# An encoder layer on one core: VectorE's wide additions and subtractions of SBUF operands issued with an accumulator output

## The chip, the cores and the metric

The kernel runs on one core of a Trainium2 chip. The metric is the device time of one execution in microseconds (us), the median of 3 runs. Engines: TensorE (PE, matrix products), VectorE (DVE), ScalarE (ACT), GpSimd (POOL) and SyncE (SP, which issues most of the DMAs).

## The reference

One layer of a streaming encoder, for a prompt of 1024 frames and for 32 new frames whose 512 predecessors are in caches. Shared weights, model width 1024, 8 + 8 heads of 64, inner width 4096, all float32:

```python
h = rmsnorm(x, g_mix)
q_a, k_a, v_a, q_i, k_i, w_i, q_b, k_b, v_b, gate_a, gate_b = split(h @ w_in)
# mixer A: q_a, k_a normed and rotated; an indexer scores every earlier frame,
score = sum_h relu(q_i @ k_i.T) * w_i         # the best 256 (sample: 136) are attended
# mixer B: stick-breaking attention, strictly causal
a = exp(log_sigmoid(z) - tail)
m = sigmoid(gate_a) * (o_a @ w_branch_a) + sigmoid(gate_b) * (o_b @ w_branch_b)
h = x + m @ w_out
y = h + square(relu(rmsnorm(h, g_ffn) @ w_up)) @ w_down
```

The outputs are y and the new keys and values of both mixers, for both groups.

## The kernel before, in words

Activations lie transposed, features on the 128 partitions and the 1056 frames (1024 + 32) along the columns. A float32 product is made of three matmuls on halves: x = xh + xl and w = wh + wl, where xh is x rounded to the matmul's type fp32r and xl the rest. `three` (L500) issues xh·wh, xl·wh and xh·wl into one PSUM bank. The halves are made by two engines: ScalarE casts (`copy`) into the high half, and VectorE or GpSimd subtracts it from the source to give the low half, both operands in SBUF. For a tile of weights (128 x 512) these are the names wst or raw (as loaded), wh and wl; rb is a second such source. GpSimd does most of the weights' subtractions in the first stages and VectorE a part of them.

The stages: the input projections and the indexer (to about 450 us, interleaved), attention of both mixers per head, then `branch`, `out` and the feed-forward part for the frames in two groups of columns, g1 (512 columns) and g2 (544 columns, in chunks of 272). The feed-forward part of g2 is computed with 7 products of quarter matrices in place of 8, so it adds and subtracts weights and activations beforehand (names rw, sl, more, il, gl, ul); sums of weights are made earlier and kept in DRAM (ws, dw_up, dw_down).

Three places that the following speaks of:

- `project_a` (L1247) makes the queries and keys of mixer A. Of each chunk of columns it squares the projection (sq), adds the squares of both halves of a head on GpSimd, casts the sum on ScalarE into the first half of a tile az and subtracts on VectorE into the second (L1301). TensorE sums over the head's rows with small matmuls `t<-heads,az` of 4 columns, first on the high half, then on the low one.
- `branch` (L1623) is the multiplication with the branch matrices. For mixer A its `done` multiplies on VectorE (pb<-pj,sg), adds the other branch on GpSimd (pb<-pb,y), casts on ScalarE (xh<-pb) and subtracts on VectorE (xl<-pb,xh, L1647). The tiles of these halves, mh and ml, lie in xh1 and xl1. Each of 8 row blocks e has two chunks of 272 columns.
- `out` (L1652) is the product with W_out: for each of 8 blocks of output rows and each chunk it accumulates over k = 0..7, and so needs the row blocks k of `branch`. k = 6 and 7 are the last that `branch` makes.

No instruction is issued where it is written. Every call goes through the class `Plan`: `record` (L303) notes the instruction, its rank and its dependences; `cost` (L237) gives its length by a formula of its engine, operation and columns; `run` and `issue` (L379, L414) then write the order, engine by engine: what is ready by the planner's own clock, the lowest rank first (URGENT, FAST, PREP, MAIN, FILL, SLOW), then the order of recording. All instructions therefore have line L436, that of the call in `issue`. The planner also keeps the shared access of VectorE and GpSimd to SBUF: `locks` (L294) says whether a VectorE instruction needs it (every GpSimd instruction does), and `issue` shifts an instruction behind the other engine's one that has it. In `cost`, a plain addition of n columns has 150 + 1.06 n ns, `tensor_tensor_reduce` 230 + 1.05 n, and `locks` says no for the latter. While `dense` is set (the feed-forward part of g2), VectorE's costs of operands outside PSUM are taken 1.3 times.

`tensor_tensor_reduce` is used in two places before the change: in `softmax_weights` (p<-s,mask; s in PSUM), and in the indexer's selection (L1142, pen<-pen,score; both in SBUF), whose accumulator outputs are read by later work.

Of the kernel before, what the change touches and what calls it, by code (L numbers as in the profile page):

```python
# [9 lines left out]
F32 = mybir.dt.float32  # L10
F32R = mybir.dt.float32r
# [3 lines left out]
ALU = mybir.AluOpType  # L15
# [72 lines left out]
class Mem:  # L88


    def __init__(self, parts, words, old=(), floor=0.0):
        self.writer = np.full((parts, words), -1, np.int32)
        self.readers = []
        self.old, self.floor = old, floor
        self.touched = []
# [14 lines left out]

TABLE = {AF.Exp: "exp", AF.Sigmoid: "sigmoid", AF.Sqrt: "sqrt"}
PE, DVE, ACT, POOL, SP = range(5)
SLACK, STORE = 300, 1000
CHANGE = 20


class Plan:
# [3 lines left out]
    def __init__(self, nc, tc):  # L121
        self.nc, self.tc = nc, tc
        self.tensor, self.vector = Issuer(self, PE, nc.tensor), Issuer(self, DVE, nc.vector)
        self.scalar, self.gpsimd = Issuer(self, ACT, nc.scalar), Issuer(self, POOL, nc.gpsimd)
        self.sync = Issuer(self, SP, nc.sync)
        self.nodes, self.mem, self.rings = [], {}, {}
        self.members, self.banks, self.onchip = {}, set(), set()
        self.floors = {"left": 0.0, "right": 0.0, None: 0.0}
        self.free = [0.0] * 5
        self.now = [[] for _ in range(5)]  # L130
        self.later = [[] for _ in range(5)]
        self.pipe = 0.0
        self.port = {DVE: (0.0, 0.0), POOL: (0.0, 0.0)}
        self.table = None
        self.row = None
        self.patience = 0
        self.level = [2]
        self.hold = None
        self.dense = False


    @contextmanager
# [94 lines left out]
    def cost(self, eng, op, out, ins, scalar, kw):  # L237
        n = 1
        for s in out.shape[1:]:
            n *= s  # L240
        if eng == PE:
            rhs = ins[1]
            cols = 1
            for s in rhs.shape[1:]:
                cols *= s
            stat = 1
            for s in ins[0].shape[1:]:
                stat *= s
            four = 4 if op == "matmul" and rhs.dtype == F32 else 1
            occ = four * max((cols + 29) / 2.4, stat / 1.2 + 2 if stat > 64 else 60)  # L250
            return occ, occ + 175
        if eng == DVE:
            if op == "reciprocal":
                d = 160 + 6.2 * n
            elif op == "tensor_tensor_scan":
                d = 160 + 2.06 * n
            elif op in ("tensor_scalar", "tensor_scalar_mul"):
                d = 160 + 1.0 * n + (80 if "accum_out" in kw else 0)
            elif op == "tensor_tensor_reduce":
                d = 230 + 1.05 * n  # L260
            elif op == "scalar_tensor_tensor":
                d = 155 + (1.06 if isinstance(scalar, (int, float)) else 1.2) * n
            elif op == "reduce_sum":
                k = 1
                for s in ins[0].shape[1:]:
                    k *= s
                d = 150 + 1.05 * k
            elif op == "memset":
                d = 100 + 0.3 * n
            elif op == "tensor_copy":  # L270
                d = 160 + 0.62 * n
            else:
                d = 150 + 1.06 * n
            if self.dense and not any(x.tensor.name in self.banks for x in ins):
                d *= 1.3
            return d - 70, d
        if eng == ACT and op != "dma_start":
            d = 195 + 0.84 * n + (190 if "accum_out" in kw else 0)
            if op == "activation" and any(not isinstance(kw.get(k, 0.0), (int, float)) for k in ("scale", "bias")):
                d += 100  # L280
            return d - 90, d
        if op == "dma_start" and eng == POOL:
            return 1000.0, 1000.0
        if eng == POOL:
            d = 300 + 0.9 * n if op in ("tensor_scalar", "memset") else 330 + 1.9 * n
            if op == "tensor_scalar" and out.dtype == F32R:
                d = 230 + 3.2 * n
            if self.dense:
                d *= 1.05
            return d - 30, d  # L290
        d = 470.0 if out.shape[0] > 64 else 620.0
        return d, d
# [9 lines left out]

    def record(self, eng, fn, op, args, kw):  # L303
        args = list(args)
        out = kw["out"] if "out" in kw else args[0]
        outs = [out] + ([kw["accum_out"]] if kw.get("accum_out") is not None else [])
        rest = args[1:] if "out" not in kw else args
        ins = [x for x in rest if isinstance(x, bass.AP)]
        ins += [x for k, x in kw.items() if isinstance(x, bass.AP) and k not in ("out", "accum_out")]
        reads = list(ins)  # L310
        if op == "copy_predicated":
            reads.append(out)
        n = Node()
        n.id, n.eng, n.call = len(self.nodes), eng, (fn, args, kw)
        n.key = (self.level[-1], n.id)
        n.occ, n.lat = self.cost(eng, op, out, ins, args[2] if op == "scalar_tensor_tensor" else None, kw)
        n.size = 0
        n.table = TABLE.get(args[2]) if op == "activation" else None
        n.store = op == "dma_start" and out.tensor.name not in self.onchip and self.level[-1] != FAST
        if op == "dma_start":  # L320
            n.size = 4
            for s in max((out, ins[0]), key=lambda z: z.size()).shape:
                n.size *= s
            if (out if out.tensor.name in self.onchip else ins[0]).shape[0] <= 64:
                n.size *= 1.6
        n.lock = eng == POOL or eng == DVE and self.locks(op, out, ins, args)
        n.row = out.tensor.name if eng == PE and self.level[-1] == FILL else None
        n.wait = self.patience
        n.succ, n.need, n.ready, n.end, n.start = [], 0, 0.0, None, None
        self.nodes.append(n)  # L330
        deps = set()
        found = []
        for aps, write in ((reads, False), (outs, True)):
            for ap in aps:
                c = self.cells(ap)
                if c is None:
                    continue
                m, part, idx = c
                w = m.writer[part, idx]
                if (w < 0).any():  # L340
                    deps.update(m.old)
                    n.ready = max(n.ready, m.floor)
                deps.update(np.unique(w).tolist())
                if write:
                    for r, rpart, ridx in m.readers:
                        if rpart.start < part.stop and part.start < rpart.stop and self.meet(idx, ridx, m.writer.shape[1]):
                            deps.add(r)
                found.append((m, part, idx, write))
        for m, part, idx, write in found:
            if write:  # L350
                m.writer[part, idx] = n.id
                if m.writer.shape == (1, 1):
                    m.readers = []
            else:
                m.readers.append((n.id, part, idx))
            if not m.touched or m.touched[-1] != n.id:
                m.touched.append(n.id)
        if eng == SP and self.hold is not None:
            deps.add(self.hold)
        deps.discard(-1)  # L360
        deps.discard(n.id)
        for d in deps:
            d = self.nodes[d]
            if d.end is not None:
                n.ready = max(n.ready, self.after(d, n))
            else:
                d.succ.append(n)
                n.need += 1
        if not n.need:
            heapq.heappush(self.later[eng], (n.ready, n.id))  # L370
# [74 lines left out]
class Layer:  # L445
# [114 lines left out]
    def run(self):  # L560
        nc, a = self.nc, self.a
# [8 lines left out]
        c = lambda shape, dt, name: nc.tile(self.const, shape, dt, name)  # L570
# [14 lines left out]
        self.vl = c([128, 4, 8], F32, "vl")  # L585
        self.gf = c([128, KB], F32, "gf")
        self.ngf = c([128, KB], F32, "ngf")

        dt = lambda shape, name: nc.tile(self.dram, shape, F32, name)
        self.dq = dt([2 * H, 2, HD, T], "dq")  # L590
# [1807 lines left out]
```

## Time and profile before

| | |
|---|---|
| median of 3 runs | 1673.52 us (1671.99 to 1674.35) |
| profiled execution | 1678.86 us, of which the span is 1677.1 |
| granted TensorE clock | 0.999 of full speed |
| busy: TensorE | 1662.6 us |
| busy: VectorE, 2577 instructions | 1212.8 us |
| busy: ScalarE | 1086.8 us |
| busy: GpSimd | 1061.6 us |

Times in the views are us from the span's start unless marked ns. A row of the timeline gives start, duration, engine, line, operation, output<-inputs, the shape (partitions x columns), and in brackets how long the engine had been idle and what ended that. A row of the groups gives the count, the busy time in all, the mean ns of one, and the idle time ahead with its releaser. In names, numbers of tiles are left out; they stand in the rows of the order below.

### The profile page before, as it was taken

How to read it: one execution, taken by the hardware profiler on the slowest of the kernel's cores; microseconds unless marked ns; L12 is line 12 of the kernel's file. 1: busy time of each engine (PE TensorE's matmuls, PEld its weight loads, DVE VectorE, ACT ScalarE, POOL GpSimd, SP SyncE). 2: the span in 40 equal slices, each digit the busy share in tenths (PEclk: the TensorE clock that was granted, in tenths of full speed). 3: DMA queues.
4: the chain of work that ended last, by engine and by line, in shares of the span. 5: the costliest groups of instructions: out<-in, count | busy, mean ns of one | idle time of the engine just before them, and what ended most of it. 6: DMA issues, size and time to landing. Idle time of an engine off the chain costs nothing.

```text
span 1677.1 us, 34259 instructions
## 1 busy us (share of the span) xinstructions
PE 1662.6 (99%) x11584; PEld 1564.8 (93%) x11584; DVE 1212.8 (72%) x2577; ACT 1086.8 (65%) x2389; POOL 1061.6 (63%) x914
## 2 busy tenths in 40 slices
PE   9999999999999999999999999999999999999999
PEld 9999999898999998989888889999999999999998
DVE  6557778999947656899888766676646783767577
ACT  7656698893235577667677666576844775747472
POOL 3366676876555266563576567778877884646563
PEclk9999999999999999999999999999999999999999
DMA  7378797745377679666597375657865656565664
GB/s 253 118 208 276 256 291 253 253 167 175 127 238 192 173 203 244 201 186 188 173 314 249 120 236 159 210 170 222 281 200 169 202 166 183 170 179 167 177 204 156
DMA packets 208339, 339.96 MB, mean 203 GB/s; under 512 B 32650, under 2 KB 62202, under 8 KB 208163
## 3 DMA queue, kind: packets, MB, share of 16 engines
q1 hardware_dynamic: 207874, 337.64, 66.1%
q8 instruction: 91, 1.49, 0.4%
q14 instruction: 86, 0.70, 0.1%
q10 hardware_dynamic: 288, 0.13, 0.0%
HBM read 249.80 MB, written 87.77 MB: 201 GB/s over the span
## 4 chain that ended last, share of the span: by engine, by line
PE 92%; DVE 5%; ACT 1%; issue 1%; POOL 1%; DMA 0%; SPq 0%; DVEq 0%; POOLq 0%; ACTq 0%
PE pj L436 65%; PE s L436 13%; PE o L436 5%; PE t L436 5%; PE pd L436 4%; DVE p L436 1%; DVE junk L436 0%; ACT junk L436 0%; DVE az L436 0%; DVE t L436 0%; DVE sl L436 0%; DVE rwq L436 0%; DVE pj L436 0%; DVE pre L436 0%; DVE more L436 0%
## 5 line engine op out<-in xcount | busy, mean ns | idle before, releaser
L436 PE MATMUL pj<-xh,wh 128*128 128x272 f32 (+2 forms) x1624 | 527.3, 326 | 3.5 <-ACT part L436 3.2
L436 PE MATMUL pj<-xl,wh 128*128 128x272 f32 (+2 forms) x1624 | 527.0, 326 | 0.0
L436 PE MATMUL pj<-xh,wl 128*128 128x272 f32 (+2 forms) x1624 | 526.7, 325 | 0.0
L436 POOL TENSOR_TENSOR wl<-wst,wh 128x512 fp32r<-128x512 f32 (+1 forms) x232 | 325.6, 1408 | 224.8 <-ACT wh L436 191.3
L436 PEld LDWEIGHTS pj<-xh,wh 128*128 128x128 f32 x1624 | 305.9, 189 | 23.6 <-ACT part L436 3.4
L436 PEld LDWEIGHTS pj<-xl,wh 128*128 128x128 f32 x1624 | 306.2, 189 | 19.1
L436 PEld LDWEIGHTS pj<-xh,wl 128*128 128x128 f32 x1624 | 305.9, 189 | 19.2
L436 ACT CAST wh<-wst 128x512 fp32r<-128x512 f32 (+1 forms) x260 | 160.0, 619 | 147.8 <-PE pj L436 107.2
L436 POOL TENSOR_TENSOR wl<-raw,wh 128x512 fp32r<-128x512 f32 x77 | 104.8, 1364 | 43.5 <-ACT wh L436 43.2
L436 PE MATMUL pj<-gl,wh 128*128 128x272 f32 (+1 forms) x444 | 126.8, 286 | 0.0
L436 PE MATMUL pj<-gh,wh 128*128 128x272 f32 (+1 forms) x444 | 126.6, 286 | 0.0
L436 PE MATMUL pj<-gh,wl 128*128 128x272 f32 (+1 forms) x444 | 126.2, 286 | 0.0
L436 DVE TENSOR_TENSOR tt<-t,tt 128x512 fp32r<-128x512 f32 (+2 forms) x168 | 101.2, 620 | 32.4 <-ACT tt L436 30.9
L436 ACT ACTIVATE junk<-score,cand 128x384 bf16<-128x384 f32 (+1 forms) x124 | 116.0, 936 | 6.0 <-DVE cand L436 4.0
L436 ACT CAST tt<-t 128x512 fp32r<-128x512 f32 (+2 forms) x168 | 87.2, 538 | 38.6 <-PE o L436 18.4
L436 ACT CAST wh<-raw 128x512 fp32r<-128x512 f32 x122 | 75.9, 624 | 53.0 <-PE pj L436 30.6
L436 DVE TENSOR_TENSOR_SCAN p<-p,seen 128x384 f32<-128x384 f32 (+3 forms) x64 | 104.7, 1659 | 4.5 <-ACT p L436 4.4
L436 PE MATMUL o<-tt,v 128*128 128x256 f32 (+1 forms) x640 | 102.7, 279 | 1.1 <-DVE o L436 1.0
L436 PEld LDWEIGHTS o<-tt,v 128*128 128x128 f32 x640 | 94.0, 189 | 10.2 <-DVE o L436 1.3
L436 POOL TENSOR_TENSOR ws<-ws 128x512 f32<-128x512 f32 x64 | 83.0, 1297 | 20.1 <-issue 8.8
L436 PE MATMUL s<-k,q 128*128 128x384 f32 (+5 forms) x384 | 93.9, 350 | 0.0
L436 PE MATMUL t<-ident,p 128*128 128x128 f32 x596 | 89.9, 274 | 0.0
(509 smaller groups left out, 4505.3 us busy)
## 6 DMA issues: line engine op xcount, KB each, us to landing
q<-dq SPq DMA_DIRECT2D x64, 256.0 KB, 4.1
raw<-w_down SPq DMA_DIRECT2D x51, 256.0 KB, 3.0
ws<-w_up SPq DMA_DIRECT2D x48, 256.0 KB, 4.4
dw_up<-ws SPq DMA_DIRECT2D x48, 256.0 KB, 3.4
k<-dk SPq DMA_DIRECT2D x48, 256.0 KB, 4.7
v<-dv SPq DMA_DIRECT2D x48, 256.0 KB, 3.7
raw<-dw_up SPq DMA_DIRECT2D x45, 256.0 KB, 3.0
wst<-w_up SPq DMA_DIRECT2D x44, 256.0 KB, 2.9
```

What stands on the lines that cost most here:

```text
L436: fn(*args, **kw)
```

## The change

In `record`, VectorE's `tensor_add` and `tensor_sub` of two-dimensional tiles of at least 256 columns, with no operand in PSUM, are issued as `tensor_tensor_reduce`: the same addition or subtraction elementwise into the same output, and a running maximum over the columns into one column of a new constant tile, `low`. Nothing reads `low`, and the planner isn't told that it is written. The planner then costs and places these instructions by its rules for `tensor_tensor_reduce`, without shared access and without the factor 1.3.

```diff
+COUNTED = {"tensor_add": ALU.add, "tensor_sub": ALU.subtract}
+LEAST, ROUNDED = 256, True
...
-            if self.dense and not any(x.tensor.name in self.banks for x in ins):
+            if self.dense and op != "tensor_tensor_reduce" and not any(x.tensor.name in self.banks for x in ins):
                 d *= 1.3
...
     def record(self, eng, fn, op, args, kw):
         args = list(args)
+        if eng == DVE and op in COUNTED and self.junk is not None:
+            out, x, y = args
+            if len(out.shape) == 2 and out.shape[1] >= LEAST and not any(z.tensor.name in self.banks for z in args):
+                if out.dtype != F32R or ROUNDED:
+                    fn, args = self.nc.vector.tensor_tensor_reduce, []
+                    kw = dict(out=out, in0=x, in1=y, scale=1.0, scalar=0.0, op0=COUNTED[op], op1=ALU.max,
+                              accum_out=self.junk[:out.shape[0]])
+                    op = "tensor_tensor_reduce"
         out = kw["out"] if "out" in kw else args[0]
-        outs = [out] + ([kw["accum_out"]] if kw.get("accum_out") is not None else [])
+        acc = kw.get("accum_out")
+        outs = [out] + ([acc] if acc is not None and (self.junk is None or acc.tensor.name != self.junk.tensor.name) else [])
...
+        nc.junk = c([128, 2], F32, "low")[:, 0:1]
```

259 of VectorE's instructions are concerned: 91 make low halves of weights wl, about 40 low halves xl of activations, 50 sums of weights, 23 more, 16 sl, 12 az, and the rest gl, ha, il and the like. Each becomes two instructions, in the order's words `ISA wl,low<-wst,wh 128x512` and `ISA low 128x1`, the second of which writes the accumulator to `low`. VectorE's instructions in the order are 2735 in place of 2476. The other engines' numbers are the same, but the order is planned anew: of the instructions that stand elsewhere in the order, outside the longest common sequence, TensorE has about 1,400 of some 11,575 (by up to 122 places), VectorE and ScalarE about 420 each, GpSimd about 130, and SyncE 246 (by up to 22 places), nearly all from 290 us on.

Two places, first the product with W_out for g2, at about 1284 us. TensorE before: k = 4 and 5 of the bank pj_16882 (first chunk of one block of output rows), and the beginning of pj_16885 (the second chunk); xh1 and xl1 are the halves of the activations, wh_16880 and wl_16881 the weights of k = 4 to 7.

```order
L436 MATMUL pj_16882<-xh1_227,wh_16880 128x272
L436 MATMUL pj_16882<-xl1_228,wh_16880 128x272
L436 MATMUL pj_16882<-xh1_227,wl_16881 128x272
L436 MATMUL pj_16882<-xh1_227,wh_16880 128x272
L436 MATMUL pj_16882<-xl1_228,wh_16880 128x272
L436 MATMUL pj_16882<-xh1_227,wl_16881 128x272
L436 MATMUL pj_16885<-xh1_227,wh_16877 128x272
L436 MATMUL pj_16885<-xl1_228,wh_16877 128x272
```

TensorE now, the same place from k = 5 on; the numbers of the tiles are 4 higher (pj_16886 is the first chunk's bank, pj_16889 the second's) and the activations are xh1_228 and xl1_229.

```order
L448 MATMUL pj_16886<-xh1_228,wh_16884 128x272
L448 MATMUL pj_16886<-xl1_229,wh_16884 128x272
L448 MATMUL pj_16886<-xh1_228,wl_16885 128x272
L448 MATMUL pj_16886<-xh1_228,wh_16884 128x272
L448 MATMUL pj_16886<-xl1_229,wh_16884 128x272
L448 MATMUL pj_16886<-xh1_228,wl_16885 128x272
L448 MATMUL pj_16889<-xh1_228,wh_16881 128x272
L448 MATMUL pj_16889<-xl1_229,wh_16881 128x272
L448 MATMUL pj_16889<-xh1_228,wl_16882 128x272
L448 MATMUL pj_16889<-xh1_228,wh_16881 128x272
L448 MATMUL pj_16886<-xh1_228,wh_16884 128x272
L448 MATMUL pj_16889<-xl1_229,wh_16881 128x272
```

Before, the second chunk starts right after k = 5 of the first, and k = 6 of the first begins 26 matmuls later; now k = 6 follows k = 5 at once, and the first matmul of k = 7 stands four matmuls into the second chunk. GpSimd before, at the same place: pb_16865 and pb_16867 are the two chunks of `branch` that become k = 6, pb_16873 and pb_16875 those of k = 7; the rows wl split weights.

```order
L436 TENSOR_TENSOR wl_16892<-wst_16890,wh_16891 128x512
L436 TENSOR_TENSOR wl_16900<-wst_16898,wh_16899 128x512
L436 TENSOR_TENSOR pb_16865<-pb_16865,y1_16204 128x272
L436 TENSOR_TENSOR pb_16867<-pb_16867,y1_16204 128x272
L436 TENSOR_TENSOR pb_16873<-pb_16873,y1_16204 128x272
L436 TENSOR_TENSOR wl_16903<-wst_16901,wh_16902 128x512
L436 TENSOR_TENSOR pb_16875<-pb_16875,y1_16204 128x272
```

GpSimd now, tile numbers again 4 higher (y1 is 5 lower).

```order
L448 TENSOR_TENSOR pb_16869<-pb_16869,y1_16199 128x272
L448 TENSOR_TENSOR pb_16871<-pb_16871,y1_16199 128x272
L448 TENSOR_TENSOR wl_16896<-wst_16894,wh_16895 128x512
L448 TENSOR_TENSOR pb_16877<-pb_16877,y1_16199 128x272
L448 TENSOR_TENSOR pb_16879<-pb_16879,y1_16199 128x272
L448 TENSOR_TENSOR wl_16904<-wst_16902,wh_16903 128x512
```

The additions of k = 6 now stand ahead of both splits of weights, and those of k = 7 between them.

The second place is `project_a` at about 319 us. TensorE before: t_4191 sums az_4190 with the matrix heads; s_4224 and s_4225 are the projections in progress.

```order
L436 MATMUL s_4224<-xh0_225,wl_4216 128x512
L436 MATMUL t_4191<-heads_74,az_4190 128x4 x4
L436 MATMUL t_4191<-heads_74,az_4190 32x4 x2
L436 MATMUL s_4225<-xh0_225,wh_4218 128x512
L436 MATMUL s_4225<-xl0_226,wh_4218 128x512
L436 MATMUL s_4225<-xh0_225,wl_4219 128x512
```

TensorE now, where az_4191 and t_4192 are the same tiles.

```order
L448 MATMUL t_4192<-heads_74,az_4191 128x4
L448 MATMUL s_4226<-xh0_226,wh_4219 128x512
L448 MATMUL s_4226<-xl0_227,wh_4219 128x512
L448 MATMUL s_4226<-xh0_226,wl_4220 128x512
L448 MATMUL s_4226<-xh0_226,wh_4219 128x512
L448 MATMUL s_4226<-xl0_227,wh_4219 128x512
L448 MATMUL s_4226<-xh0_226,wl_4220 128x512
L448 MATMUL s_4226<-xh0_226,wh_4219 128x512
L448 MATMUL s_4226<-xl0_227,wh_4219 128x512
L448 MATMUL s_4226<-xh0_226,wl_4220 128x512
L448 MATMUL t_4192<-heads_74,az_4191 128x4 x3
L448 MATMUL t_4192<-heads_74,az_4191 32x4 x2
```

Nine matmuls of the next projection now stand between the first of the small sums and the rest. In VectorE's order the subtraction that makes the low half of this az stands two counting passes of the indexer's selection later than before.

More of the change, by code (lines that the diff above doesn't have):

```diff
@@ L139, in __init__ @@
         self.dense = False
+        self.junk = None
     @contextmanager
```

## Prediction

> **What bounds the kernel now.** I read the page first: the engines' busy time, the granted clock, and the chain that ended last.
>
> ```profile
> PE 1662.6 (99%) x11584; PEld 1564.8 (93%) x11584; DVE 1212.8 (72%) x2577; ACT 1086.8 (65%) x2389; POOL 1061.6 (63%) x914
> ...
> PEclk9999999999999999999999999999999999999999
> ...
> PE 92%; DVE 5%; ACT 1%; issue 1%; POOL 1%; DMA 0%; SPq 0%; DVEq 0%; POOLq 0%; ACTq 0%
> ```
>
> TensorE is busy for 1662.6 us at full clock, and the change neither removes nor shortens a matmul. VectorE has 28% of the span free. So a cheaper addition on VectorE pays only where TensorE waits for it. The waits of TensorE come next: who was waited for, the sum in us, how often, the longest.
>
> ```profile
> PE pj L436 <- ACT part L436: 3.2, 1, 3.2
> PE s L436 <- DVE t L436: 2.6, 3, 1.2
> PE t L436 <- DVE az L436: 2.0, 2, 1.3
> PE o L436 <- DVE ss L436: 1.2, 1, 1.2
> PE o L436 <- DVE o L436: 1.0, 1, 1.0
> ```
>
> These sum to 10.0 us in 8 waits. That is the most that any change off TensorE can win: 0.6%. No row says that TensorE waited for a weight's low half wl, the largest group of the additions concerned; the weights are ready ahead of their use.
>
> **The new form itself.** The kernel already has the form with the accumulator: pen<-pen,score, a few times, with both operands in SBUF. Its instruction is named CUSTOM_DVE_ANT_0, and it is followed by a read of the accumulator. Two of them fell beside work of GpSimd. First VectorE, then GpSimd, then one pen instruction that met no GpSimd work, by the timeline (start, duration):
>
> ```profile
> 391.02 1.53 DVE L436 CUSTOM_DVE_ANT_0 pen<-pen,score 128x384 f32<-128x384 f32 x1
> 392.49 0.08 DVE L436 DVE_READ_ACCUMULATOR2_ANT lowa<- 128x1 f32 x1
> 392.49 0.51 DVE L436 SCALAR_TENSOR_TENSOR t<-s,gqk,rope_ct 128x288 f32<-128x288 f32 x1
> ...
> 395.25 1.62 DVE L436 CUSTOM_DVE_ANT_0 pen<-pen,score 128x1024 f32<-128x1024 f32 x1
> ```
> ```profile
> 390.73 1.41 POOL L436 TENSOR_TENSOR wl<-wst,wh 128x512 fp32r<-128x512 f32 x1
> ...
> 394.98 0.81 POOL L436 TENSOR_TENSOR az<-t,az 128x288 fp32r<-128x288 f32 x1 [0.54 <-ACT az L436]
> 395.83 2.19 POOL L436 TENSOR_TENSOR wl<-wst,wh 128x512 fp32r<-128x512 f32 x1
> ```
> ```profile
> 435.60 0.95 DVE L436 CUSTOM_DVE_ANT_0 pen<-pen,score 128x768 f32<-128x768 f32 x1
> ```
>
> 768 columns took 0.95 us undisturbed. The one of 384 columns is half as wide and took 1.53: GpSimd's subtraction held until 392.14, and VectorE's ended 0.41 behind that. The one of 1024 columns took 1.62: it ended at 396.87, 1.08 after GpSimd's az ended at 395.79. GpSimd's next subtraction took 2.19 instead of about 1.4, and ended 1.15 after VectorE's end. So the form with an accumulator waits for GpSimd, and GpSimd for it, as two plain subtractions do. The planner of this kernel believes otherwise: by its rules this form needs no shared access.
>
> **The change, part by part.** (1) 259 instructions get a second one, the read of the accumulator. Its price and that of the contended plain form, by the groups (busy, mean ns of one):
>
> ```profile
> L436 DVE TENSOR_TENSOR wl<-wst,wh 128x512 fp32r<-128x512 f32 x27 | 24.5, 908 | 7.3 <-ACT wh L436 6.9
> ...
> L436 DVE DVE_READ_ACCUMULATOR2_ANT mx<- 128x1 f32 x100 | 8.1, 81 | 0.0
> ```
>
> 259 x 0.081 = 21 us on VectorE at most. The read at 392.49 starts together with the next instruction, so that between nothing and all of it lies beside other work. VectorE's 28% free are 464 us, and TensorE waits 8 times. If about 4 such reads stand ahead of an awaited result it is 4 x 0.08 = +0.3, my value; 12 of them would be +1.0. [...]
>
> (2) Contention. The mean of 908 ns for 512 columns holds some waiting: the pen row of 768 columns less 256 columns at the same rate would be about 0.7 (estimate from these rows). By the two contended pen rows this waiting stays: 0. That it goes is the first rival.
>
> (3) A new wait. In W_out of g2 the order changes at k = 6 and 7 (the order rows stand with the change). What made these operands before: VectorE's multiplications and subtractions, GpSimd, ScalarE, and two matmuls of TensorE: the first of the second chunk, in whose slot k = 6 now stands, and the one with which k = 6 began:
>
> ```profile
> 1282.04 1.12 DVE L436 TENSOR_TENSOR pb<-pj,sg 128x272 f32<-128x272 f32 x3
> 1286.60 2.02 DVE L436 TENSOR_TENSOR xl<-pb,xh 128x272 fp32r<-128x272 f32 x3 [3.44 <-ACT xh L436]
> ```
> ```profile
> 1282.53 1.30 POOL L436 TENSOR_TENSOR wl<-wst,wh 128x512 fp32r<-128x512 f32 x1 [1.06 <-DVE pb L436]
> 1283.78 2.23 POOL L436 TENSOR_TENSOR pb<-pb,y 128x272 f32<-128x272 f32 x3
> ```
> ```profile
> 1286.16 1.05 ACT L436 CAST xh<-pb 128x272 fp32r<-128x272 f32 x3
> ```
> ```profile
> 1284.01 0.29 PE L436 MATMUL pj<-xh,wh 128*128 128x272 f32 x1
> ...
> 1287.27 0.29 PE L436 MATMUL pj<-xh,wh 128*128 128x272 f32 x1
> ```
>
> The two TensorE rows stand 26 matmuls and 3.26 us apart, 0.125 us for 272 columns. Before, TensorE filled the time from 1284.01 to 1287.27 with other products. In the new order k = 6 is asked for at 1284.01 and its low half at 1284.13; k = 7 is asked for seven matmuls after 1284.01, at 1284.9. VectorE's first product is there at 1282.4 as before (1282.04 + 1.12 / 3). GpSimd, which no longer has its splits in front, adds for 0.74 (2.23 / 3), ScalarE casts for 0.35 (1.05 / 3), VectorE subtracts for 0.37 alone or 0.67 (2.02 / 3) beside GpSimd, and from each engine to the next pass some 0.3: 1284.8 to 1285.1 for the low half of k = 6, or a wait of 0.7 to 1.0, and up to 1.3 more if VectorE has to let the split of 1.30 pass. For k = 7 GpSimd does two additions, one split and a third addition from 1282.7 on, 3 x 0.74 + 1.30, until 1286.2; 0.3 later ScalarE and 0.35 after that there is its high half, at 1286.9, while TensorE is ready for it at 1284.9 + 0.7 to 1.0, so that another wait of about 1.0 to 1.2 follows. I take +2.0 for both; the ends are +1.0 (one of the two falls away) and +3.0 (the split passes first).
>
> (4) A wait that may go. A subtraction az of 288 columns took 3.94 us; VectorE, GpSimd's last rows meanwhile, and TensorE behind it:
>
> ```profile
> 316.45 3.94 DVE L436 TENSOR_TENSOR az<-sq,az 128x288 fp32r<-128x288 f32 x1
> ```
> ```profile
> 317.50 1.35 POOL L436 TENSOR_TENSOR wl<-wst,wh 128x512 fp32r<-128x512 f32 x1
> 318.75 1.32 POOL L436 TENSOR_TENSOR ws<-ws 128x512 f32<-128x512 f32 x1
> ```
> ```profile
> 320.44 0.56 PE L436 MATMUL t<-heads,az 128*128 128x4 f32 x5 [1.33 <-DVE az L436]
> ```
>
> It ended at 320.39, 0.32 after GpSimd's row of 318.75 had ended at 320.07, and TensorE lost 1.33. In the new order nine matmuls of 512 columns stand between the first matmul on az (the high half) and the rest, 9 x 0.125 x 512 / 272 = 2.1 us of cover; VectorE's own order has the az two counting passes later, which gives some of it back. I take -1.3, the longer of the two az waits; the ends are 0 and -2.0, both. [...]
>
> A second such case, sl, feeds what TensorE waits longest for (the 3.2 <- ACT part):
>
> ```profile
> 1361.37 5.25 DVE L436 TENSOR_TENSOR sl<-raw,sh 128x512 fp32r<-128x512 f32 x1
> ```
> ```profile
> 1360.09 2.61 POOL L436 TENSOR_TENSOR wl<-raw,wh 128x512 fp32r<-128x512 f32 x2
> ...
> 1364.61 1.46 POOL L436 TENSOR_TENSOR acc<-acc,y 128x544 f32<-128x544 f32 x1
> ```
>
> VectorE got through only when GpSimd's run of work ended at 1366.07. The new order leaves VectorE's row there as it was, and GpSimd's run as long, so that the 3.2 stay: 0.
>
> (5) All other moved instructions. Of some 11,575 matmuls about 1,400 are elsewhere in the order, by up to 122 places, from about 290 us on. Nothing in the trace shows these waits. They can't win over 10.0. On the other side a few places like (3) would cost 2 each, up to +10. The order is written by a planner for an accumulator form that needs no turn with GpSimd, which the pen rows contradict: so a small loss is nearer than a gain, less than one more place like (3): +1.5.
>
> The sum: +0.3 + 0 + 2.0 - 1.3 + 1.5 = +2.5. The profiled execution's own time is 1678.86 (span 1677.1), 5.3 above the median of 1673.52; it becomes 1681.4, and the median 1673.52 + 2.5 = 1676.0. The ends of terms 1, 3 and 4 give from -1.0 to +4.0 before term 5 is varied; with 3 either way on that term's +1.5 it is -2.5 to +8.5, so the likeliest case lies between 1671 and 1682.
>
> **The rivals.** *The form needs no turn with GpSimd* for these operands. Then both az waits go (-2.0), the wait behind sl too (-3.2), the three waits for t (2.6), which follow such subtractions on VectorE, are halved (-1.3), and the new wait shrinks to +1.0: -5.5, 1668. Against it stand the rows of 1.53, 1.62 and 2.19; for it, that these are only two meetings. Chance 0.12.
>
> *The new order is worse throughout*, the slower end. TensorE's order was drawn up for subtractions that never wait; where the operand comes late, all matmuls behind it wait, as at 1284. It decides from two or three further places on: with five in all and 2.0 each it is 10 - 1.3 (az) + 0.3 (reads) = +9.0: 1682.5. For it: 1,400 moved matmuls, the shifted order of GpSimd beside them; against it, that TensorE's work on weights runs several us behind their preparation. Chance 0.28.
>
> [...] Chance 0.03. [...]
>
> **How the numbers follow.** The likeliest case has 0.57. A measurement of this kernel can tell about 0.2%, 3.3 us, from no change: below 1670.2 is faster, above 1676.9 slower. The likeliest case divides into 0.06 faster, 0.36 same and 0.15 slower; the first rival into 0.10 and 0.02 same; the second is slower but for 0.01, 0.27; half rate 0.03. That gives faster 0.16, same 0.39, slower 0.45. The range reaches down to the first rival, 1668, and up over the second, 1685; beyond it lie about 0.05 below and 0.1 above. The likeliest case's own range is 1671 to 1682.
>
> **What would show it.** Right: the new wl instructions of 512 columns keep a mean near 0.9 us, reads of 0.08 stand behind each, GpSimd's busy time stays at about 1060, TensorE's waits lose the az of 1.33 and gain one of 1 to 3 us for xl or xh in W_out, and sl's wait is still there. [...] I am wrong if the waits on TensorE fall clearly below 10, or if TensorE's busy time itself moves.

## The result and the profile after

The changed kernel takes 1687.67 us in the median of 4 runs (1686.09 to 1691.95) against 1673.4 before: ratio 1.0088, with a 95% interval of 1.0070 to 1.0106. It is 14.3 us slower, 2.7 beyond the upper end of the range. The profiled execution took 1686.92.

The page of the changed kernel, the engines' busy time:

```profile
PE 1668.8 (99%) x11584; PEld 1565.6 (93%) x11584; DVE 1214.4 (72%) x2836; ACT 1085.8 (64%) x2389; POOL 1061.5 (63%) x914
```

GpSimd and ScalarE do what they did. VectorE has 259 more instructions and is 1.6 us busier. TensorE executes the same matmuls and yet is busy for 6.2 us longer, which the prediction named as a sign of its being wrong. The waits of TensorE, as before:

```profile
PE s L448 <- DVE t L448: 2.2, 1, 2.2
PE s L448 <- DVE lowa L448: 2.1, 1, 2.1
PE pj L448 <- DVE y L448: 1.8, 2, 1.2
PE t L448 <- DVE low L448: 1.4, 2, 1.0
PE o L448 <- DVE ss L448: 1.2, 1, 1.2
PE o L448 <- DVE o L448: 1.1, 2, 0.8
PE pj L448 <- ACT xh L448: 0.7, 2, 0.4
...
PE pj L448 <- DVE xl L448: 0.2, 1, 0.2
```

The 3.2 for part, behind sl, are gone. In their place stand waits that were not there: 2.1 behind the indexer's lowa, 1.8 for y, and one of 2.2 for t where there were three of 2.6 together. With the rows left out they sum to 11.6 against 10.0, so that waiting alone explains little of the 14.3. What follows one of them is seen in the matmuls (start, duration):

```profile
339.41 0.40 PE L448 MATMUL pj<-xh,wl 128*128 128x512 f32 x1
342.03 0.57 PE L448 MATMUL s<-xh,wh 128*128 128x288 f32 x1 [2.22 <-DVE t L448]
342.40 0.44 PE L448 MATMUL s<-xl,wh 128*128 128x288 f32 x1
342.64 0.44 PE L448 MATMUL s<-xh,wl 128*128 128x288 f32 x1
...
345.52 0.30 PE L448 MATMUL s<-xh,wl 128*128 128x288 f32 x1
345.66 0.29 PE L448 MATMUL s<-xh,wh 128*128 128x288 f32 x1
```

After the wait the matmuls of 288 columns follow one another every 0.24 us, from 342.40 to 345.52, and then every 0.14. The granted clock of that stretch, in a table of windows (busy time of PE, PEld, DVE, ACT, POOL, then the clock), first after, then before:

```profile
340.00:350.00 10.00, 7.97 (x47) 7.70 (x48) 8.64 (x29) 8.99 (x20) 7.53 (x8) 0.83 0.66 211
```
```profile
340.00:350.00 10.00, 10.00 (x72) 9.55 (x71) 9.55 (x31) 9.30 (x21) 8.59 (x9) 1.00 0.73 242
```

For 3.4 us the granted clock was about half (0.51 from 342.03 to 345.50), which counts as busy time: 1.7 us (10 x 0.17) on top of the wait. Why it fell after this wait the traces don't show: after the 2.1 for lowa, at 394.68, it stayed at 1.00.

So 1.7 of the 6.2 us of busy time are the clock. The rest is seen in two kernels of the next section, tile_only (only the new tile) and order_only (the new order and the tile, plain instructions); both traces run at full clock up to the last matmul:

```profile
PE 1663.8 (99%) x11584; PEld 1564.2 (93%) x11584; DVE 1205.7 (72%) x2577; ACT 1087.3 (65%) x2389; POOL 1060.3 (63%) x914
```
```profile
PE 1667.3 (99%) x11584; PEld 1566.3 (93%) x11584; DVE 1211.7 (72%) x2577; ACT 1085.5 (65%) x2389; POOL 1064.8 (63%) x914
```

The tile adds 1.2 us to TensorE's busy time and the order 3.5. With the clock's 1.7 that is 6.4, near the 6.2. Which matmuls take longer isn't worked out here; the list of waits holds nothing under 0.15 us.

What the same 259 instructions cost, by the groups of the changed kernel, three of the wl and the reads:

```profile
L448 DVE CUSTOM_DVE_ANT_0 wl<-raw,wh 128x512 fp32r<-128x512 f32 x45 | 41.5, 923 | 13.4 <-ACT wh L448 12.1 <-POOL wl L448 0.2
...
L448 DVE CUSTOM_DVE_ANT_0 wl<-wst,wh 128x512 fp32r<-128x512 f32 x27 | 22.9, 848 | 5.9 <-ACT wh L448 5.3
...
L448 DVE DVE_READ_ACCUMULATOR2_ANT low<- 128x1 f32 x257 | 20.4, 79 | 0.0
...
L448 DVE CUSTOM_DVE_ANT_0 wl<-rb,wh 128x512 fp32r<-128x512 f32 x16 | 13.3, 831 | 4.0 <-ACT wh L448 3.6
```

Two of these groups before, by the same view:

```profile
L436 DVE TENSOR_TENSOR wl<-raw,wh 128x512 fp32r<-128x512 f32 x45 | 37.2, 829 | 12.7 <-ACT wh L436 9.2 <-DMA rb<-w_up 2.6
...
L436 DVE TENSOR_TENSOR wl<-rb,wh 128x512 fp32r<-128x512 f32 x16 | 12.8, 797 | 5.0 <-ACT wh L436 3.8 <-issue 0.8
```

With the 24.5 of wl<-wst shown in the prediction, the 88 took 74.5 us before and take 77.7 now. By these means the form waits for GpSimd as the plain instruction does; the reads, 20.4 us, come to it.

### The profile page after: what moved, and what is told of

Read it like the earlier page. It is cut to its first block, busy times and chain, and to the rows that moved or that the text cites. A ratio compares the mean times of both kernels' runs of the same rounds, so it can differ in the third digit from the quotient of the medians.

```text
span 1685.1 us, 34575 instructions
## 1 busy us (share of the span) xinstructions
PE 1668.8 (99%) x11584; PEld 1565.6 (93%) x11584; DVE 1214.4 (72%) x2836; ACT 1085.8 (64%) x2389; POOL 1061.5 (63%) x914
```

## The experiments

Theory 1: the order is the cause, since it was planned in the belief that 259 instructions need no turn with GpSimd. Theory 2: the form itself costs it. Theory 3: any newly planned order costs about that much. Theory 4 came up on the way: the new tile low moves everything behind it in SBUF.

**Form and order apart.** form_only, against the changed kernel, so that the planner still sees a plain operation:

```diff
-                    op = "tensor_tensor_reduce"
```

> The 259 instructions are issued in the form with the accumulator, but the planner costs and places them as the plain additions they were, so that every engine has the order of before (VectorE with 259 reads of the accumulator between). Theory 1, the new order under a wrong belief on the shared access makes the loss of 14 us: 1673.4 to 1675, the reads lie beside other work. Theory 2, the form itself makes it (each result is released 0.08 us later, 20 us more on VectorE): 1683 or more. Theory 3, any newly planned order costs that much: as theory 1 here.

Measured: 1679.14, ratio 1.0028 (1.0017 to 1.0039). order_only keeps the order that the planner made for the new form, and the tile low, but issues the plain instruction:

```diff
-                    fn, args = self.nc.vector.tensor_tensor_reduce, []
-                    kw = dict(out=out, in0=x, in1=y, scale=1.0, scalar=0.0, op0=COUNTED[op], op1=ALU.max,
-                              accum_out=self.junk[:out.shape[0]])
```

> The order of the changed kernel, drawn up for the form with the accumulator, but the 259 instructions are issued as plain additions and subtractions, without reads. Theory 1: 1685 to 1688. Theory 2: 1672 to 1676. Theory 3: 1685 to 1688.

Measured: 1684.30, 1.0060 (1.0047 to 1.0073), just under the 1685 of theories 1 and 3. The order makes most of the 0.88% and the form a smaller part; neither theory 1 nor theory 2 had that for form_only. The two parts seem to add up, 0.60 + 0.28 = 0.88, but both kernels have the tile low, so that its share is in both numbers.

**The planner told.** told_lock is the changed kernel with

```diff
-        return op not in ("tensor_tensor_reduce", "reduce_sum", "reciprocal", "memset")
+        return op not in ("reduce_sum", "reciprocal", "memset")
```

> The changed kernel, with the planner told that the form needs its turn with GpSimd (costs as changed); the order is planned anew. Theory 1, the belief that the form needs no turn is what spoils the order: 1673 to 1677. Theory 2: 1685 or more, as the form is the same. Theory 3, before's order is one of the better ones and any other is worse: 1680 to 1690.

Measured: 1675.77, 1.0007 (0.9999 to 1.0016), as theory 1 has it. Theory 3 stood against it with nudge_up, in the kernel before:

```diff
-                d = 150 + 1.06 * n
+                d = 155 + 1.06 * n
```

> The kernel before, but the planner's cost of VectorE's plain operations is 155 + 1.06 n ns in place of 150 + 1.06 n; nothing else. The order is planned anew, by beliefs that are no worse than before. Theory 1: 1671 to 1677. Theory 2: 1671 to 1677. Theory 3: 1680 to 1690.

Measured: 1683.16, 1.0051 (1.0039 to 1.0063). A change of 5 ns in a cost, with the same beliefs, loses 8.7 us by the order that comes of it. So theory 3 was not out: this is its range.

**The tile.** tile_only is the kernel before with one line, and the order of before on every engine:

```diff
+        c([128, 2], F32, "low")
```

> The kernel before, with nothing added but the constant tile low of 2 columns, which here nobody writes or reads. The order is that of before on every engine. The tile takes 32 bytes of each partition, so that the tiles behind it on the left side, the halves of activations and weights among them, begin 32 bytes later, at odd multiples of 32 in place of multiples of 64. Theory 4, the shifted addresses slow the matmuls (the mean pitch of the 512-column ones was 230.0 ns in the two runs without the tile and 230.6 to 230.8 in the four with it): 1676.5 to 1678.5. Theory 2, the form itself makes the 4.6 us of the run form_only: 1673 to 1675.

Measured: 1676.34, 1.0012 (1.0003 to 1.0021), between the two ranges. Three more kernels have 64 bytes in place of 32, by `c([128, 16], F32, "low")`. The first, form_aligned, is form_only with that:

> As form_only (259 instructions in the form with the accumulator, the order of before), but the tile low has 16 columns, 64 bytes, so that what lies behind it keeps its place modulo 64. Theory 4: 1674 to 1676, and a 512-column pitch of 230.0 ns. Theory 2: 1678 to 1680, as form_only.

Measured: 1677.58, 1.0018 (1.0008 to 1.0027). after_aligned is the changed kernel with it:

> The changed kernel with the tile low of 16 columns; order and instructions as changed. Theory 4: 3 to 4 us off the changed kernel's 1687.7, 1683 to 1685; the rest, 10, is the order's. Theory 2: 1686 to 1688.

Measured: 1686.76, 1.0071 (1.0058 to 1.0083). told_aligned is told_lock with it:

> As told_lock (the planner told that the form needs its turn with GpSimd) with the tile of 16 columns. Theory 4: 1672 to 1673, a little faster than before. Theory 2: 1675 to 1677, as told_lock.

Measured: 1677.64, 1.0018 (1.0009 to 1.0027), slower than told_lock, where theory 4 had it faster. None of the four times falls into theory 4's range.

The traces show an effect of the tile all the same. The mean distance from the start of a 512-column matmul to the start of the next matmul (distances under 300 ns, all of a trace) is 230.0 to 230.2 ns without the tile, 230.6 to 230.8 with 32 bytes and 230.2 to 230.4 with 64. The 0.6 ns on 1900 matmuls are 1.2 us. In the times the alignment is not settled: two of the three pairs gain 0.10 and 0.17% by it, the third loses 0.11, and each is uncertain by 0.12 to 0.22. What stands is that the tile alone costs 0.12% (0.03 to 0.21). With it taken off once from each number above, the form costs 0.16% (uncertain by 0.14) and the order 0.48% (by 0.16). Order, form and tile then make 0.76 of the 0.88%; the missing 0.12 is within the uncertainty.

**The belief, with costs held equal.** told_plain has the order of told_lock with plain instructions and no tile.

> The order of told_lock (planned with the costs of the form and with its turn with GpSimd), but the 259 instructions are plain additions and subtractions and the tile low isn't there. Sum of the parts measured so far: told_lock stands at +0.07%, of which the form and the tile are +0.28%, so that its order should give -0.2%: 1670 to 1672.5. If the parts don't add up: 1674 to 1677.

Measured: 1671.80, 0.9982 (0.9971 to 0.9993), as expected if the parts add up. nudge_down is nudge_up with 145:

> The kernel before, the planner's cost of VectorE's plain operations 145 + 1.06 n ns in place of 150 + 1.06 n. Theory 1, an order is spoilt by the belief that the 259 need no turn with GpSimd, and nudge_up was an unlucky draw: 1671 to 1677. Theory 3, each newly planned order scatters by some 10 us whatever the beliefs: anything from 1671 to 1686, 1678 to 1684 the likeliest.

Measured: 1682.82, 1.0049 (1.0034 to 1.0064): another draw (a newly planned order) that loses by right beliefs. no_lock is the kernel before with one belief changed, wide being the test that `record` makes in the change:

```diff
-        n.lock = eng == POOL or eng == DVE and self.locks(op, out, ins, args)
+        n.lock = eng == POOL or eng == DVE and not wide and self.locks(op, out, ins, args)
```

> The kernel before, but the planner believes that the 259 additions and subtractions need no turn with GpSimd (their costs as before, the factor 1.3 kept, issued as plain instructions). Theory 1: 1681 to 1686. Theory 3: anything from 1671 to 1686.

Measured: 1683.65, 1.0054 (1.0038 to 1.0070). no_lock_235 has besides

```diff
+        if wide:
+            d = 235 + 1.05 * out.shape[1]
+            n.occ, n.lat = d - 70, d
```

> Plain instructions, no tile low, the planner's belief of the changed kernel (no turn with GpSimd, no factor 1.3) with costs of 235 + 1.05 n in place of 230 + 1.05 n. Theory 1: 1681 to 1686. Theory 3: anything from 1671 to 1686.

Measured: 1682.54, 1.0047 (1.0031 to 1.0063). no_lock_225 is the same with 225; told_225 and told_235 have these costs (and so no factor 1.3) with the line n.lock of before.

> Plain instructions, the planner told that the 259 need their turn with GpSimd, their cost 225 + 1.05 n without the factor 1.3. Theory 1, the belief decides: 1670 to 1677. Theory 3, each new draw scatters, and told_plain was a good one: anything from 1671 to 1686, 1680 to 1684 the likeliest.

Measured: 1669.95, 0.9975 (0.9964 to 0.9986). told_235:

> As told_225 with 235 + 1.05 n. Theory 1: 1670 to 1677. Theory 3: anything from 1671 to 1686, 1680 to 1684 the likeliest.

Measured: 1672.97, 0.9993 (0.9984 to 1.0002). no_lock_225:

> Plain instructions, the planner's wrong belief (no turn with GpSimd, no factor 1.3) with costs of 225 + 1.05 n. Theory 1: 1681 to 1686. Theory 3: anything from 1671 to 1686, 1680 to 1684 the likeliest.

Measured: 1684.59, 1.0060 (1.0048 to 1.0072). nudge_160 is one more draw by right beliefs:

> The kernel before with the planner's cost of VectorE's plain operations at 160 + 1.06 n in place of 150 + 1.06 n. Theory 1: 1671 to 1677. Theory 3: anything from 1671 to 1686, 1680 to 1684 the likeliest.

Measured: 1677.22, 1.0013 (1.0003 to 1.0023).

In each of the first four rows of this table only the belief differs; the instructions are plain and the costs the same (ratios to the kernel before):

| planner's cost of the 259 | right belief | wrong belief |
|---|---|---|
| 150 + 1.06 n | 1 (before) | 1.0054 (no_lock) |
| 225 + 1.05 n | 0.9975 (told_225) | 1.0060 (no_lock_225) |
| 230 + 1.05 n | 0.9982 (told_plain) | 1.0048 (order_only less the tile's 0.12%) |
| 235 + 1.05 n | 0.9993 (told_235) | 1.0047 (no_lock_235) |
| 145, 155, 160 + 1.06 n | 1.0049, 1.0051, 1.0013 (nudge_down, nudge_up, nudge_160) | not run |

Four times of four the wrong belief costs 0.5 to 0.9%. In the last two pairs the halves ran on different chips, each beside the kernel before. With the new form in place it is the same: the changed kernel is 0.81% over told_lock, after_aligned 0.53% over told_aligned. So theory 1 is shown for these costs. Theory 3 holds as a second thing: two of the seven orders planned by right beliefs, those at 145 and 155, lose as much. Why these lose was not tried.

What the wrong belief does is seen in the waits of TensorE. All seven traces whose first part was planned by it (the changed kernel, after_aligned, order_only, no_lock, no_lock_225, no_lock_235 and early_wrong, which follows) have a wait of 1.6 to 2.7 us behind the indexer's lowa; none of the other 13 has one. nudge_up and nudge_down haven't, so that they lose by something else.

**Where it is lost.** Two last kernels give told_225 the wrong belief in one part only:

```diff
+        n.lock = eng == POOL or eng == DVE and not (wide and not self.dense) and self.locks(op, out, ins, args)
```

> As told_225 (plain instructions, costs 225 + 1.05 n), but in the part before the quarter products (dense not set, to about 1000 us) the planner believes that the 259 need no turn with GpSimd. The traces of told_225 and no_lock_225 are 8.2 us apart at matmul 6250 and 14.3 at the end. Theory 1 with the loss in both parts: about 8 over told_225, 1677 to 1679, and TensorE waits for t and lowa at 330 to 400 us. If the loss were one place's only: 1670 or 1684.

Measured: 1680.28, 1.0039 (1.0026 to 1.0052), 0.64% over told_225, more than expected. late_wrong has `wide and self.dense`:

> As told_225, with the wrong belief only where dense is set (from about 1000 us); the order up to matmul 6257 is that of told_225. Theory 1 with the loss in both parts: about 6 over told_225, 1675 to 1677, with TensorE's waits for y at 1040 to 1140 us. If the loss were one place's only: 1670 or 1684.

Measured: 1672.90, 0.9991 (0.9982 to 1.0000), 0.16% over told_225 (uncertain by 0.14), less than expected; its trace has the expected waits for y, 1.8 us. Together 0.80%, near the pair's 0.85: four fifths of it arise before 1000 us. TensorE in the stage of the indexer's selection, told_225 first, then early_wrong (windows):

```profile
340.00:350.00 10.00, 10.00 (x79) 9.78 (x78) 9.59 (x31) 9.21 (x20) 8.79 (x10) 1.00 0.63 216
390.00:400.00 10.00, 10.00 (x65) 8.95 (x64) 9.37 (x20) 3.82 (x10) 7.55 (x8) 1.00 0.63 215
```
```profile
340.00:350.00 10.00, 8.01 (x48) 7.74 (x49) 8.76 (x28) 9.09 (x21) 7.69 (x8) 0.83 0.63 211
390.00:400.00 10.00, 7.36 (x27) 5.64 (x26) 9.86 (x24) 2.01 (x5) 5.97 (x7) 0.83 0.49 168
```

And TensorE's two long waits in early_wrong:

```profile
PE s L443 <- DVE lowa L443: 2.6, 1, 2.6
PE s L443 <- DVE t L443: 2.2, 1, 2.2
```

Two waits of 4.8 us together, each followed by 1.7 us at a reduced clock, make 8.2. The same matmul, number 2500, starts at 398.2 in told_225 and at 406.6 in early_wrong: 8.4 apart. So up to there waits and clock close the sum of this execution. By the last matmul the two traces are 12.4 apart; where the other 4 arise is not worked out here. And the clock's share changes from one execution to the next: another execution of early_wrong, with a granted clock of 1.0, still took 1679.14, 9.2 above told_225. In order_only, whose order is that of the changed kernel, a wait of 2.6 for t at the same place was followed by no slow stretch.

## Why the prediction was wrong

It went the way that was forecast, but by +14.3 against +2.5, and the range ended at +11.5. By its steps:

**Term 5, all other moved instructions, +1.5, is the step that failed.** It was put at less than one more place like the one in W_out, because nothing in the trace before showed such waits. The order alone cost 0.48%, 8 us (5 to 11), where terms 3, 4 and 5 had +2.2 for it together; as 3 and 4 came to nothing (below), the 8 are term 5's. The trace of order_only is 7.9 longer than that of tile_only (spans of 1682.5 and 1674.6): the waits sum to 11.1 against 6.3, and TensorE's busy time is 3.5 higher. So the premise failed too that the waits are the most that a change off TensorE can move: TensorE's busy time moves with the order as well.

The second rival, the new order worse throughout, was nearest: +9.0. It was given 0.28. Its number is in part luck, since it counted on five waits of 2.0, and two came (2.2 and 2.1), with 11.6 for all waits together. The reason written for the small value, "a planner for an accumulator form that needs no turn", was the cause, as the pairs show. How it looks, VectorE after, at the long wait:

```profile
339.24 0.86 DVE L448 TENSOR_SCALAR_CACHE_REDUCE junk<-score,cand 128x640 bf16<-128x640 f32 x1
...
340.14 0.77 DVE L448 TENSOR_SCALAR_CACHE_REDUCE junk<-score,cand 32x544 bf16<-32x544 f32 x1
...
341.11 0.48 DVE L448 SCALAR_TENSOR_TENSOR t<-s,gqk,rope_ct 128x256 f32<-128x256 f32 x1
341.50 0.48 DVE L448 SCALAR_TENSOR_TENSOR t<-s,gqk,rope_st 128x256 f32<-128x256 f32 x1
```

The t, whose end frees the PSUM bank that TensorE waits for, stands behind two counting passes of the indexer's selection, which have the lowest rank. None of the 259 stands in this stretch. The last one ahead of it, an az of 512 columns at 331.68, took 1.70 where 768 ns were planned, but an az of that width took 1.70 in told_225 as well (at 331.34), and TensorE did not wait for t. That points to the place in the order and not to the length. And in the feed-forward part of the first group, VectorE, GpSimd, and TensorE:

```profile
1129.83 1.43 DVE L448 CUSTOM_DVE_ANT_0 raw<-rb 128x512 f32<-128x512 f32 x1
...
1131.30 1.65 DVE L448 CUSTOM_DVE_ANT_0 rb<-raw,rb 128x512 f32<-128x512 f32 x1
...
1132.88 0.41 DVE L448 TENSOR_TENSOR y<-y,pj 128x256 f32<-128x256 f32 x1
```
```profile
1128.97 3.43 POOL L448 TENSOR_TENSOR wl<-raw,wh 128x512 fp32r<-128x512 f32 x2
```
```profile
1133.34 0.51 PE L448 MATMUL pj<-us,wh 128*128 128x256 f32 x2 [1.19 <-DVE y L448]
```

Two sums of weights were placed ahead of the y that TensorE waits for. Their planned length is 230 + 1.05 x 512 = 768 ns each; they took 1.43 and 1.65 beside GpSimd's two subtractions, 1.5 more than planned, and TensorE stood 1.19.

**Term 1, the reads, +0.3, was probably too small.** The form alone costs 0.16%, 2.7 us, uncertain by 2.4. That 8 waits of TensorE leave little room for it was the reason given; where the 2.7 arise the traces don't show, since the one trace of form_only ends no later than that of tile_only (last matmul 1669.8 and 1670.4).

**Not in the sum at all: the tile low.** It costs 0.12%, 2.0 us, with an unchanged order. With the order's 8.0 and the form's 2.7 that is 12.7 of the 14.3 us.

**Term 2, contention unchanged, was right.** In one order the 259 take the same in both forms: 235.9 us in all as plain instructions (the trace of tile_only) and 237.1 in the form (form_only), reads left out. The wl of 512 columns have the same median before and after, 0.69 us. The first rival, a form that needs no turn, is out. So is half rate, the chance of 0.03, a form that takes nearly twice the plain instruction's time: the shortest of these wl took 0.63 us in the form and 0.68 as a plain subtraction before.

**Term 3, W_out, +2.0, did not come.** No wait of TensorE stands there. VectorE's product for k = 6 after, and its matmul:

```profile
1288.08 0.44 DVE L448 TENSOR_TENSOR pb<-pj,sg 128x272 f32<-128x272 f32 x1 [0.47 <-PE pj L448]
```
```profile
1294.64 0.29 PE L448 MATMUL pj<-xh,wh 128*128 128x272 f32 x1
```

The operand is begun 6.6 us ahead of its use; before, it was 2.0 us (1282.04 and the slot at 1284.01). The working took "as before" for VectorE, while the new order had moved its operands earlier too. The 0.3 from each engine to the next was an estimate and too long: in the trace before GpSimd's addition at 1289.12 starts 0.14 after VectorE's product of 1288.55 has ended, and ScalarE's cast at 1289.92 starts 0.03 after that addition.

**Term 4, the az wait, -1.3, was credited to the wrong account.** The 3.94 of az and the 5.25 of sl belong to the profiled execution and not to the order. With the same order, in tile_only:

```profile
316.53 0.69 DVE L436 TENSOR_TENSOR az<-sq,az 128x288 fp32r<-128x288 f32 x1
...
1362.01 0.68 DVE L436 TENSOR_TENSOR sl<-raw,sh 128x512 fp32r<-128x512 f32 x1
```

These two stalls cost TensorE 1.3 and 3.2, most of the 5.3 by which that execution lies above the median. So the median, as it seems, did not hold them (single executions behind it have no trace), and nothing could be won from it. The cover came as predicted: in the changed kernel neither az wait of before is left, but two others of 1.0 and 0.3 us stand at 413 and 435.

## What to carry to other kernels

Where a planner writes the order, a change of an instruction's cost or locks is first of all a change of the order: split it into form and order by two kernels before reading waits, and compare orders by pairs that differ in one belief, since a cost moved by 5 ns made 0.5% here. A belief that the traces contradict (that an operation needs no turn with GpSimd, where two sums of 512 columns took 1.43 and 1.65 us beside it and the wl of that width 0.69 in the median) cost 0.5 to 0.9% in four pairs; a right belief doesn't protect from a bad order, though. The fastest order of all, 1669.95 us, 0.25% below the kernel before, came from the plain instructions with right beliefs and the cost 225 + 1.05 n. And when the profiled execution lies above the median, look for stalls that only it has before any saving is booked on them.

## What the runs showed of the hardware

- The 20 traces hold 17 waits of TensorE of 2.0 to 3.2 us. After 7 of them the granted clock was near half for some 3.4 us (once twice that, told_aligned at 541), which costs 1.7 us; after the other 10, the wait of 3.2 at 1366 before among them, it was not. A wait of 1.7 was followed by it too (nudge_160 at 860). So in these traces the length of the wait alone doesn't decide.
- In the trace before two VectorE subtractions with both operands in SBUF ended only behind three GpSimd instructions that had begun later than they (from 316.74 and from 1362.58 on): an az of 288 columns took 3.94 us and an sl of 512 columns 5.25, where they took 0.69 and 0.68 in tile_only. It is rare: of 14 traces with plain instructions 4 have one over 2.1 us among the 259 (two in the kernel before, 5.25 and 3.94), of the 6 traces with the form none has one over 1.9. Whether the form is spared or these were lucky is open.
